# A two-layer MLP in Strassen form: one unit's split operands stay in SBUF, and the second product takes that unit first

## The chip, the cores and the metric

The kernel runs on one core of a Trainium2 chip. The time is the device time of one execution in microseconds (us), and less is better. The names of the engines in the profile are PE (TensorE's matmuls), PEld (its weight loads), DVE (VectorE), ACT (ScalarE), POOL (GpSimd) and SP (SyncE, which here only issues transfers).

## What is computed

One layer of a transformer trunk over 1024 tokens of width 1024, in float32. The part that this document is about is its last line but one, the MLP:

```python
mix = hybrid_mixer(x, w_in, b_f, pool_w, pool_scale, w_out)   # pooling heads and gated attention
x = layer_norm(ALPHA * x + mix, ln1_g, ln1_b)
hid = jnp.square(jax.nn.relu(x @ w_mlp1))                     # 1024 x 1024 by 1024 x 4096
x = layer_norm(ALPHA * x + hid @ w_mlp2, ln2_g, ln2_b)        # 1024 x 4096 by 4096 x 1024
```

## The kernel before

**Splits.** A float32 matrix is split into a high part in fp32r (a cast on ScalarE) and a low part (the rest, by a subtraction on VectorE); `split` at L70 does both, and a product is then three matmuls, high by high, high by low and low by high. In the profile L71 is the cast and L72 the subtraction.

**Seven products.** Both MLP products are done in two-by-two blocks with seven block products in place of eight, named p1 to p7 throughout. Each adds into one PSUM bank (`bank`, L63; banks have the tags s, pt, pv and mm). p1, p6, p7 and p4 of one unit or step run one after the other into the same bank and p5 and p3 into another, and between them the bank is emptied into SBUF, so that each next product must wait for that.

**The first product.** `Unit` u, 0 to 15, makes two column blocks of the hidden layer for both halves of the tokens. Its seven products have 12 matmuls each (128 x 128 by 128 x 512). It leaves four results in tiles of the tag A: `ra` and `rb` (after relu and square), and `sa` and `sb`, sums of them. `out_r` (L682) and `out_s` (L688) split these and write high and low parts to `hid_dram` from POOL's queue, seven writes of 512 KB a unit: the pair A12/A11, the pair S1/S2, the pair S3/S4 (two writes each, L680), and A22 (one, L686).

**The second product.** `Step` s is one of four quarters q = s % 4 of the tokens (128 of the first and 128 of the second half), and takes the hidden units in `TAKES[s]` (L851); every unit is taken once in each quarter. For a unit taken a product is three matmuls, so that a step with four units has seven products of 12 matmuls. `load` (L864) reads the units' operands of that quarter from `hid_dram` into tiles of the tags Q or A: three reads of 256 KB and one of 128 KB for each unit. `Pair` u holds the weights of unit u: two loads of 512 KB into tiles of the tag S (`load_f`, `load_g`), four sums on VectorE and seven splits into tiles of the tag B. Each step adds its products into `y` (`into`, L900): on the first four steps p1, p6, p5 and p4 are copied there by ScalarE (L903), and the rest, and all later ones, are added by VectorE (L905); p2 stays in a bank of its own to the last four steps. Before, steps 0, 1, 2 and 3 take 1, 2, 3 and 4 units, steps 4 to 11 four, and the last seven 3, 3, 3, 4, 4, 3 and 2; there are 19.

**Order.** The program writes the order out by hand: `chain` (L962) is units 2 to 15 and then the steps, and the loop at L1006 puts the products of one member (p1, p2, p6, p5) between those of the one before it (p7, p3, p4), so that unit 15's last three products lie among step 0's first four. `at(i, place, ...)` (L965) hangs loads, splits and outputs at places 0 to 7 of that order. The framework then sorts each engine's instructions by this order, and puts one forward where the engine would stand idle; it also gives out the slots. Each tag has a fixed number of them (L48: S 3, U 2, B 14, Q 10, A 9), and a tile waits until a slot's last user is done, which for a tile written to DRAM is the landing of the write. While the first product runs its operands `A[...]` fill all 14 B slots.

The numbers of the lines that the prediction speaks of: L895 the second product's matmul, L573 the first one's, L641, L646, L629 its evacuations by ScalarE, L657 to L664 its relu and square, L667 to L672 its sums, L677 and L678 the split of a result to be written, L874 the reads of `hid_dram`, L804 and L808 the loads of a pair.

Of the kernel before, what the change touches and what calls it, by code (L numbers as in the profile page):

```python
# [14 lines left out]
P = 128  # L15
# [9 lines left out]
NF = FF // P  # L25
# [9 lines left out]

@with_exitstack
def trunk(ctx, tc, xT, xn, wuqk, wvf, bf, poolw, pscale, wout, g1, b1, w1, w2, g2, b2, out):


# [11 lines left out]
    def slot(tag, shape, dt=F32R):  # L51
        uid[0] += 1
        return sb.tile([P] + list(shape), dt, tag=tag, bufs=NBUF[tag], name=f"{tag}{uid[0]}")
# [9 lines left out]
    def bank(tag=None):  # L63
        uid[0] += 1
        if tag is None:
            tag = CYCLE[rr[0] % 8]
            rr[0] += 1
        return ps.tile([P, CH], F32, tag=tag, bufs=PBUF[tag], name=f"{tag}{uid[0]}")

    def split(hi, lo, src):  # L70
        nc.scalar.copy(hi, src)  # L71
        nc.vector.tensor_tensor(lo, src, hi.bitcast(F32), ALU.subtract)  # L72
# [39 lines left out]
    def load_x(c, kp):  # L112
        st = slot("Q" if c == 0 else "S", [2, CH], F32)
        for k in range(2):
            if c == 0 and kp == 0:
                nc.sync.dma_start(st[:, k], xT[c, kp, :, k])
            elif k == 0:
                nc.sync.dma_start(st, xT[c, kp])
            if k == 0:
                x = slot("B", [2, 2, CH])  # L120
            t = x[:, k]
            split(t[:, 0], t[:, 1], st[:, k])
            xs[c, 2 * kp + k] = t
# [3 lines left out]
    def load_wvf(kp):  # L127
        st = slot("S", [2, 2 * VW], F32)
        hi, lo = slot("A", [2, 2 * VW]), slot("A", [2, 2 * VW])
        wv.append((hi, lo))  # L130
        if kp:
            nc.sync.dma_start(st, wvf[kp])
        for k in range(2):
            pieces = [slice(0, VW), slice(VW, 2 * VW)] if kp == 0 and k == 0 else [slice(0, 2 * VW)]
            for c in pieces:
                if kp == 0:
                    nc.sync.dma_start(st[:, k, c], wvf[kp, :, k, c])
                split(hi[:, k, c], lo[:, k, c], st[:, k, c])
                yield
# [22 lines left out]
    for kp in range(4):  # L162
        g = load_wvf(kp)
        if kp == 0:
            next(g)
        load_x(0, kp)
        for _ in g:
            pass
# [14 lines left out]
    for t in range(4, NT):  # L183
        for half in range(2):
            b = bank()[:, 0:VW]
# [274 lines left out]
    GROUPS = (("A12", "A11"), ("S1", "S2"), ("S3", "S4"), ("A22",))  # L460
# [14 lines left out]
    def load_row(tag, src):  # L475
        t = slot(tag, [D], F32)
        nc.sync.dma_start(t, src.to_broadcast([P, D]))
        return t

    class Norm:  # L480


        def __init__(self, y, gam, bet, store):
            self.y, self.gam, self.bet, self.store = y, gam, bet, store
            self.cols = [slice(0, CH), slice(CH, D)]
            self.st = small([P, 2, 6], "bns", bufs=4)
            self.mv, self.rt = small([P, 2], "mv", bufs=4), small([P, 5], "rt", bufs=4)
# [47 lines left out]
    A = {b: (slot("B", [H, CH]), slot("B", [H, CH])) for b in ("A11", "A12")}  # L535
    R0, R1, A22, raw22 = {}, {}, {}, {}
# [33 lines left out]
    def product(dst, b, a, first):  # L570
        for k in range(H):
            for i, (x, y) in enumerate(((0, 0), (0, 1), (1, 0))):
# [2 lines left out]
                    stop=k == H - 1 and i == 2, skip_group_check=not first,  # L575
                )

    class Unit:


        def __init__(self, u):
            self.u, self.v = u, {}

        def load_f(self):
            self.f = slot("S", [2, H, P], F32)
            nc.sync.dma_start(self.f.rearrange("p b k f -> p (b k) f"), w1[2 * self.u])
# [28 lines left out]
        def split_t2(self):  # L615
            v = slot("Q", [2, 1, H, P])
            self.keep(("T2",), v[:, 0], v[:, 1], self.t2.rearrange("p (o k) f -> p o k f", o=1))
# [55 lines left out]

        def out(self, name, x):

            hi = slot("A", [4, 2, P])
            nc.scalar.copy(hi, x)  # L677
            nc.vector.tensor_tensor(x, x, hi.bitcast(F32), ALU.subtract)  # L678
            for i, part in enumerate((hi.bitcast(F32), x)):
                nc.gpsimd.dma_start(hid_dram[self.u, :, i, AT[name] : AT[name] + 2 * CH], part.rearrange("p q n t -> p (q n t)"))  # L680

        def out_r(self):  # L682
            self.out("A12", self.ra)
            w = slot("A", [2, 4, P])
            split(w[:, 0], w[:, 1], self.rb[:, :, 1])
            nc.gpsimd.dma_start(hid_dram[self.u, :, :, AT["A22"] :], w.bitcast(F32).rearrange("p h q t -> p h (q t)"))  # L686

        def out_s(self):  # L688
# [3 lines left out]
    NU = NF // 2  # L692
    units = [Unit(u) for u in range(NU)]
    last = None
    for m in range(4):
# [13 lines left out]
        for t in (2 * m, 2 * m + 1):  # L709
# [11 lines left out]
            for n, part in enumerate(yp):  # L721
                ns = slice(n * CH, (n + 1) * CH)
                for k in range(KT):
                    a = mh[k // 4]
# [71 lines left out]
    class Pair:  # L796
# [29 lines left out]
            tt(f[:, 1], g[:, 1], f[:, 1], ALU.add)  # L826

        def split_t2(self):
            i = self.u % 4
            if self.u in (0, 2):  # L830
                t2b[i // 2] = slot("B", [2, 2, CH])
            w = t2b[i // 2][:, i % 2]
            self.put("T2", w[:, 0], w[:, 1], self.t2)
# [11 lines left out]
            self.both(("T4", "B22"), self.g)  # L845

    pairs = [Pair(u) for u in range(NU)]
    nh = [0]


    TAKES = [range(max(0, s - 3), s + 1) for s in range(12)]  # L851
    TAKES += [range(9, 12), range(10, 13), range(11, 14), range(12, 16), range(12, 16), range(13, 16), range(14, 16)]
    NS = len(TAKES)
    FIRST = [min(s for s in range(NS) if u in TAKES[s]) for u in range(NU)]

    class Step:


        def __init__(self, s):
            self.s, self.q, self.us = s, s % 4, list(TAKES[s])  # L860
            self.first, self.final, self.end = s < 4, s >= NS - 4, s == NS - 1
            self.h = {}

        def load(self, names):  # L864

            n = len(names)
            o = AT[names[0]] + self.q * n * P
            per = 4 // n
            for a in range(0, len(self.us), per):
                us = self.us[a : a + per]  # L870
                h = slot("A" if nh[0] >= 15 and (nh[0] - 15) % 11 > 7 else "Q", [per, 2, n, P])
                nh[0] += 1
                for e, u in enumerate(us):
                    nc.sync.dma_start(h[:, e].bitcast(F32).rearrange("p h n t -> p h (n t)"), hid_dram[u, :, :, o : o + n * P])  # L874
                    for k, name in enumerate(names):
                        self.h[u, name] = h[:, e, :, k]
# [4 lines left out]

        def load_x(self):

            self.t = self.s - 4
            self.xr = slot("S", [D], F32)
            nc.sync.dma_start(self.xr, x1_dram[self.t])

# [2 lines left out]

        def prod(self, dst, a, b, first):
            for u in self.us:
                h, w = self.h[u, a], pairs[u].v[b]
                for j, (p_, q_) in enumerate(((0, 0), (0, 1), (1, 0))):
                    nc.tensor.matmul(  # L895
                        dst, h[:, p_], w[q_], start=first and u == self.us[0] and j == 0,
                        stop=u == self.us[-1] and j == 2, skip_group_check=not first,
                    )
# [66 lines left out]
    def at(i, place, *fns):  # L965
        after.setdefault((i, place), []).extend(fns)

    for i, x in enumerate(chain):
        if isinstance(x, Unit):
            if x.u >= 4:  # L970
                at(i - 1, 0, x.load_f)
                at(i - 1, 2, x.load_g)
                at(i - 1, 3, x.split_f)
                at(i - 1, 4, x.sums)
                at(i - 1, 6, x.split_t2)
            if x.u >= 3:
                at(i, 1, x.split_t14)
                at(i, 4, x.split_t3b)
            at(i + 1, 7, x.sums_s)
            at(i + 2, 1, x.out_r)  # L980
            at(i + 2, 2, x.out_s)
        else:
            for k, p in enumerate(p for p in pairs if FIRST[p.u] == x.s):
                at(i - 1, 4 * k, p.load_f)
                at(i - 1, 2 + 3 * k, p.load_g)
                at(i - 1, 3 + 3 * k, p.split_b)
                at(i - 1 + k, 4 - 3 * k, p.sums)
                at(i - 1 + k, 5 - 4 * k, p.split_t2)
                at(i, 2 + k, p.split_t13)
                at(i, 6, p.split_t4b)  # L990
            if x.first:
                at(i - 1, 4, x.room)
            if 4 <= x.s < 12:
                at(i - 1, 6, x.load_x)
                at(i, 4, x.add_x)
            for n, place in enumerate((-4, -1, 0, 2) if 1 <= x.s < 4 else (-2, 0, 2, 4)):
                at(i + (place < 0) * -1, place % 7, lambda x=x, n=n: x.load(GROUPS[n]))
            if x.s == NS - 5:
                at(i + 1, 0, lambda: rows.update(gb=(load_row("S", g2), load_row("S", b2))))
# [59 lines left out]
```

## Time and profile before

| | us |
|---|---|
| median of 3 runs | 1069.94 (1068.82 to 1071.36) |
| profiled execution | 1071.98 |
| its span, first to last instruction | 1070.2 |
| TensorE busy | 1025.5 (96%) |
| VectorE busy | 772.9 (72%) |
| ScalarE busy | 499.9 (47%) |
| GpSimd busy | 119.6 (11%) |
| moved by DMA | 202.62 MB, of it 58.73 MB by POOL's queue |

A profile is one execution with every instruction's start and length. A line of it names the source line, the engine, the operation, and the tiles without their numbers, so `s<-B,Q` is a matmul into a bank of the tag s from a B tile and a Q tile. What stands in brackets is how long the engine had been idle before, and what it was waiting for. Matmuls overlap, so a group of 12 that shows 2.88 us starts 2.72 us before the next. MLP work runs from 420 to 1055 us of the span; the second product begins at 726.

### The profile page before, as it was taken

The page shows a single profiled execution, that of the slowest core. Times are in us where ns is not written, and L with a number is a line of the kernel's source. Part 1 is how long each engine was busy: PE and PEld are TensorE (multiplying, and loading weights), DVE is VectorE, ACT ScalarE, POOL GpSimd, SP SyncE. Part 2 cuts the span into 40 slices and gives each one's busy share as a digit, 9 for nine tenths or more (in the row PEclk, how much of TensorE's full clock was granted, in tenths as well). Part 3 has the DMA queues.
Part 4 walks back from the last instruction along what each step waited for, and adds up shares of the span by engine and source line. Part 5 has one row for each costly group of instructions (what it writes and reads, how often), then busy time and mean ns, then how long its engine had stood idle before and what let it go on. Part 6 is the DMA issues. An engine that isn't in the chain of part 4 may idle for free.

```text
span 1070.2 us, 14071 instructions
## 1 busy us (share of the span) xinstructions
PE 1025.5 (96%) x5006; PEld 849.4 (79%) x5006; DVE 772.9 (72%) x1308; ACT 499.9 (47%) x799; POOL 119.6 (11%) x188
## 2 busy tenths in 40 slices
PE   7999999999989999899999999998799999999994
PEld 7988787888768788688888888886688888888883
DVE  3576677777896798779788787888555575566568
ACT  4423666566773323476766667666422221122021
POOL 0000000000000021112122121221100000000055
PEclk9999999999999999899999999999899999999997
DMA  6303311021456532248667576679989888868852
GB/s 218 102 27 106 97 50 51 19 65 43 135 149 170 168 138 79 79 153 321 233 248 267 219 279 226 255 264 320 379 287 314 275 272 276 285 214 267 256 161 106
DMA packets 116726, 202.62 MB, mean 189 GB/s; under 512 B 9576, under 2 KB 82088, under 8 KB 116656
## 3 DMA queue, kind: packets, MB, share of 16 engines
q1 hardware_dynamic: 100528, 143.00, 41.7%
q0 software_dynamic: 16128, 58.73, 14.2%
q8 instruction: 39, 0.64, 0.3%
q14 instruction: 31, 0.25, 0.1%
HBM read 130.32 MB, written 71.37 MB: 188 GB/s over the span
## 4 chain that ended last, share of the span: by engine, by line
PE 77%; DVE 9%; DMA 7%; ACT 3%; issue 2%; SPq 0%; DVEq 0%; ACTq 0%
PE s L895 15%; PE s L573 11%; PE pv L895 7%; PE mm L573 6%; PE pt L573 6%; PE pv L573 4%; PE pv L384 3%; DMA Q<-hid_dram 3%; DMA S<-rin_dram 2%; PE mm L85 2%; PE mm L83 2%; PE mm L84 2%; PE pt L895 2%; PE mm L895 2%; PE s L83 2%
## 5 line engine op out<-in xcount | busy, mean ns | idle before, releaser
L71 ACT CAST B<-S 128x1024 fp32r<-128x1024 f32 (+1 forms) x94 | 80.1, 868 | 186.1 <-DMA S<-in_w_dram 75.9
L895 PE MATMUL s<-B,Q 128*128 128x512 f32 x579 | 142.8, 398 | 9.4 <-DMA Q<-hid_dram 9.4
L895 PEld LDWEIGHTS s<-B,Q 128*128 128x128 f32 x579 | 111.5, 193 | 34.2 <-DMA Q<-hid_dram 10.7
L72 DVE TENSOR_TENSOR B<-S,B 128x1024 fp32r<-128x1024 f32 (+1 forms) x94 | 92.5, 994 | 49.1 <-ACT B L71 48.8
L573 PE MATMUL s<-B,Q 128*128 128x512 f32 x504 | 122.0, 396 | 0.6 <-ACT B L71 0.6
L573 PEld LDWEIGHTS s<-B,Q 128*128 128x128 f32 x504 | 96.4, 191 | 21.7 <-ACT B L71 1.0
L71 ACT CAST Q<-S 128x1024 fp32r<-128x1024 f32 x53 | 55.5, 1050 | 65.6 <-PE s L573 16.6
L72 DVE TENSOR_TENSOR Q<-S,Q 128x1024 fp32r<-128x1024 f32 x53 | 64.6, 1220 | 25.9 <-ACT Q L71 25.7
L573 PE MATMUL mm<-B,Q 128*128 128x512 f32 x324 | 77.7, 390 | 0.0
L680 POOL DMA_DIRECT2D hid_dram<-A x96 | 51.4, 542 | 233.4 <-ACT A L677 195.9
L895 PE MATMUL pv<-B,Q 128*128 128x512 f32 x291 | 71.5, 390 | 0.3 <-ACT Q L903 0.3
L573 PEld LDWEIGHTS mm<-B,Q 128*128 128x128 f32 x324 | 60.7, 188 | 13.2 <-DVE Q L72 0.4
L573 PE MATMUL pt<-B,Q 128*128 128x512 f32 x288 | 68.7, 389 | 0.0
L384 PE MATMUL pv<-A,B 128*128 128x256 f32 x320 | 61.5, 297 | 5.2 <-ACT A L369 3.4
L384 PEld LDWEIGHTS pv<-A,B 128*128 128x128 f32 x320 | 49.1, 188 | 21.5 <-ACT A L369 9.1
L895 PEld LDWEIGHTS pv<-B,Q 128*128 128x128 f32 x291 | 54.5, 188 | 12.1 <-ACT Q L903 0.7
L573 PEld LDWEIGHTS pt<-B,Q 128*128 128x128 f32 x288 | 54.1, 188 | 11.2
L370 DVE TENSOR_TENSOR A<-pt,A 128x512 fp32r<-128x512 f32 (+1 forms) x80 | 49.2, 634 | 16.4 <-ACT A L369 15.8
L678 DVE TENSOR_TENSOR A<-A,A 128x1024 f32<-128x1024 f32 x48 | 57.0, 1217 | 3.4 <-ACT A L677 3.4
L347 ACT ACTIVATE A<-A,nm 128x128 f32<-128x128 f32 (+3 forms) x64 | 49.7, 777 | 20.9 <-DVE nm L345 20.6
L83 PE MATMUL mm<-B,B 128*128 128x512 f32 x120 | 51.7, 431 | 0.0
L369 ACT CAST A<-pt 128x512 fp32r<-128x512 f32 (+1 forms) x80 | 41.7, 539 | 17.0 <-PE pt L368 16.2
(360 smaller groups left out, 2180.6 us busy)
## 6 DMA issues: line engine op xcount, KB each, us to landing
hid_dram<-A POOLq DMA_DIRECT2D x112, 512.0 KB, 4.2
Q<-hid_dram SPq DMA_DIRECT2D x146, 256.0 KB
S<-in_w_dram SPq DMA_DIRECT2D x63, 512.0 KB
A<-hid_dram SPq DMA_DIRECT2D x46, 256.0 KB
S<-in_wuqk_dram SPq DMA_DIRECT2D x12, 512.0 KB
Q<-hid_dram SPq DMA_DIRECT2D x47, 128.0 KB
A<-ncf_dram SPq DMA_DIRECT2D x8, 512.0 KB
S<-in_wout_dram SPq DMA_DIRECT2D x8, 512.0 KB
```

The source lines that it names most:

```text
L71: nc.scalar.copy(hi, src)
L72: nc.vector.tensor_tensor(lo, src, hi.bitcast(F32), ALU.subtract)
L83: nc.tensor.matmul(dst, a[0], b[0], start=first, stop=False)
L84: nc.tensor.matmul(dst, a[0], b[1], start=False, stop=False)
L347: nc.scalar.activation(pt[:, :nk], pt[:, :nk], AF.Exp, bias=nm, scale=-1.0, accum_out=rsum[h][:, i : i + 1])
L369: nc.scalar.copy(tt[:, 0, ev], tp[:, ev])
L370: nc.vector.tensor_tensor(tt[:, 1, ev], tp[:, ev], tt[:, 0, ev].bitcast(F32), ALU.subtract)
L384: nc.tensor.matmul(ov, V[j][:, h].rearrange("p s d -> p (s d)"), tt[:, s, a:b], start=(j == 0 and s == 0), stop=(j == 2 * m + 1 and s == 1),)
L573: nc.tensor.matmul(dst, b[x][:, k], A[a][y][:, k], start=first and k == 0 and i == 0, stop=k == H - 1 and i == 2, skip_group_check=not first,)
L678: nc.vector.tensor_tensor(x, x, hi.bitcast(F32), ALU.subtract)
L680: nc.gpsimd.dma_start(hid_dram[self.u, :, i, AT[name] : AT[name] + 2 * CH], part.rearrange("p q n t -> p (q n t)"))
L895: nc.tensor.matmul(dst, h[:, p_], w[q_], start=first and u == self.us[0] and j == 0, stop=u == self.us[-1] and j == 2, skip_group_check=no ...
```

## The change

Unit 14 (`KEPT`) no longer writes to `hid_dram`. Its results are split straight into three B tiles (A12/A11, S1/S2, S3/S4) and one A tile (A22), which stay until step 3 is done. Its outputs are hung at earlier places: the split of `ra` behind unit 15's p6, the sums and A22 behind its own p4, the rest behind unit 15's p5, where before all three stood one to two places of the chain later. The second product takes unit 14 first, alone in steps 0 and 1 and with unit 0 in step 2 and units 0 and 1 in step 3; the others follow in the order 0 to 13 and 15, two steps later than before, so there are 20 steps: 1, 1, 2, 3, 3 units, then eight of 4 and the same seven at the end. The places that go by the number of the step (loads of the residual `x`, the early places of the loads, which loads use A slots, and the two shared tiles of the T2 splits) are shifted to fit.

```diff
+    KEPT = NF // 2 - 2
     class Unit:
         def __init__(self, u):
             self.u, self.v = u, {}
+            self.kept = {} if u == KEPT else None
...
         def out(self, name, x):
+            if self.kept is not None:
+                w = slot("B", [2, 4, 2, P])
+                split(w[:, 0], w[:, 1], x)
+                for n, one in enumerate(next(g for g in GROUPS if name in g)):
+                    self.kept[one] = w[:, :, :, n]
+                return
             hi = slot("A", [4, 2, P])
...
+        def out_a(self):
+            self.out("A12", self.ra)
+
         def out_r(self):
-            self.out("A12", self.ra)
+            if self.kept is None:
+                self.out_a()
             w = slot("A", [2, 4, P])
             split(w[:, 0], w[:, 1], self.rb[:, :, 1])
+            if self.kept is not None:
+                self.kept["A22"] = w
+                return
             nc.gpsimd.dma_start(hid_dram[self.u, :, :, AT["A22"] :], w.bitcast(F32).rearrange("p h q t -> p h (q t)"))
...
         def split_t2(self):
-            i = self.u % 4
-            if self.u in (0, 2):
+            i = nt2[0] % 4
+            nt2[0] += 1
+            if nt2[0] in (1, 3):
                 t2b[i // 2] = slot("B", [2, 2, CH])
...
-    TAKES = [range(max(0, s - 3), s + 1) for s in range(12)]
-    TAKES += [range(9, 12), range(10, 13), range(11, 14), range(12, 16), range(12, 16), range(13, 16), range(14, 16)]
+    ORDER = [u for u in range(NU) if u != KEPT]
+    TAKES = [[KEPT] * (s < 4) + ORDER[max(0, s - 5) : max(0, s - 1)] for s in range(13)]
+    TAKES += [ORDER[a:b] for a, b in ((8, 11), (9, 12), (10, 13), (11, 15), (11, 15), (12, 15), (13, 15))]
...
-            for a in range(0, len(self.us), per):
-                us = self.us[a : a + per]
-                h = slot("A" if nh[0] >= 15 and (nh[0] - 15) % 11 > 7 else "Q", [per, 2, n, P])
+            loaded = [u for u in self.us if u != KEPT]
+            for a in range(0, len(loaded), per):
+                us = loaded[a : a + per]
+                h = slot("A" if nh[0] >= 11 and (nh[0] - 11) % 11 > 7 else "Q", [per, 2, n, P])
...
-            self.t = self.s - 4
+            self.t = self.q + 4 * (self.s >= 9)
...
-                h, w = self.h[u, a], pairs[u].v[b]
+                h, w = units[KEPT].kept[a][:, :, self.q] if u == KEPT else self.h[u, a], pairs[u].v[b]
...
-            at(i + 1, 7, x.sums_s)
-            at(i + 2, 1, x.out_r)
-            at(i + 2, 2, x.out_s)
+            if x.kept is None:
+                at(i + 1, 7, x.sums_s)
+                at(i + 2, 1, x.out_r)
+                at(i + 2, 2, x.out_s)
+            else:
+                at(i + 1, 5, x.out_a)
+                at(i + 1, 6, x.sums_s, x.out_r)
+                at(i + 1, 7, x.out_s)
...
-            if 4 <= x.s < 12:
+            if 5 <= x.s < 13:
...
-            for n, place in enumerate((-4, -1, 0, 2) if 1 <= x.s < 4 else (-2, 0, 2, 4)):
+            for n, place in enumerate((-4, -1, 0, 2) if 2 <= x.s < 5 else (-2, 0, 2, 4)):
```

## Rows read from the trace of the kernel before

**Rows 1.** The page, part 2: TensorE's busy tenths in 40 slices of 26.75 us.

```profile
PE   7999999999989999899999999998799999999994
```

**Rows 2.** Waits of TensorE over the whole run: total us, times, longest us.

```profile
PE s L895 <- DMA Q<-hid_dram: 9.4, 3, 6.8
```

**Rows 3.** TensorE's timeline: start, us, line, what; in brackets the idle time before.

```profile
723.41 2.88 PE L573 MATMUL pt<-B,Q 128*128 128x512 f32 x12
726.13 0.84 PE L895 MATMUL s<-B,Q 128*128 128x512 f32 x3
...
736.50 0.84 PE L895 MATMUL pv<-B,Q 128*128 128x512 f32 x3
...
741.07 0.96 PE L895 MATMUL pv<-B,Q 128*128 128x512 f32 x3 [0.33 <-ACT Q L903]
...
752.23 6.07 PE L895 MATMUL s<-B,Q 128*128 128x512 f32 x15 [6.76 <-DMA Q<-hid_dram]
758.14 2.20 PE L895 MATMUL mm<-B,Q 128*128 128x512 f32 x9
...
767.46 0.96 PE L895 MATMUL s<-B,Q 128*128 128x512 f32 x3 [0.31 <-DMA Q<-hid_dram]
770.79 6.00 PE L895 MATMUL s<-B,Q 128*128 128x512 f32 x18 [2.37 <-DMA Q<-hid_dram]
776.63 2.89 PE L895 MATMUL mm<-B,Q 128*128 128x512 f32 x12
...
799.78 2.90 PE L895 MATMUL s<-B,A 128*128 128x512 f32 x12
```

**Rows 4.** Stretches: length, each engine's busy us, granted clock, DMA share, GB/s.

```profile
705.00:726.00 21.00, 21.00 (x94) 17.38 (x94) 17.16 (x23) 15.06 (x21) 3.88 (x7) 1.00 0.74 263
726.00:737.20 11.20, 11.20 (x51) 9.04 (x50) 11.20 (x16) 9.28 (x15) 2.84 (x6) 1.00 0.87 289
737.20:745.30 8.10, 7.77 (x34) 5.88 (x32) 8.06 (x13) 5.76 (x8) 1.54 (x3) 1.00 1.02 363
745.30:752.30 7.00, 0.24 (x2) 0.07 (x1) 3.56 (x4) 3.98 (x6) 2.53 (x5) 0.88 1.04 344
752.30:758.20 5.90, 5.90 (x16) 4.73 (x17) 1.98 (x4) 0.87 (x2) 0.82 (x2) 0.57 1.06 392
758.20:771.00 12.80, 10.12 (x44) 7.78 (x43) 5.85 (x8) 5.62 (x9) 0.00 (x0) 1.00 1.06 386
...
800.00:941.00 141.00, 141.00 (x622) 116.63 (x621) 87.11 (x119) 30.23 (x39) 0.00 (x0) 1.00 0.88 282
```

**Rows 5.** Chain that ended last, 735 to 800: start, us, what.

```profile
742.68 8.38 DMA Q<-hid_dram
...
751.68 12.90 DMA Q<-hid_dram
```

**Rows 6.** VectorE's timeline, 705 to 800, same columns as rows 3.

```profile
722.75 1.23 DVE L72 TENSOR_TENSOR B<-S,B 128x1024 fp32r<-128x1024 f32 x1 [1.84 <-ACT B L71]
...
729.37 0.68 DVE L671 TENSOR_TENSOR A<-A,A 128x512 f32<-128x512 f32 x1
...
743.05 0.68 DVE L905 TENSOR_TENSOR Q<-Q,pv 128x512 f32<-128x512 f32 x1
...
744.85 1.22 DVE L678 TENSOR_TENSOR A<-A,A 128x1024 f32<-128x1024 f32 x1
```

**Rows 7.** ScalarE's timeline, 705 to 800, same columns.

```profile
729.69 0.63 ACT L71 CAST B<-S 128x512 fp32r<-128x512 f32 x1
...
740.43 0.58 ACT L903 ACTIVATE Q<-pv 128x512 f32<-128x512 f32 x1
...
747.92 0.62 ACT L71 CAST B<-S 128x512 fp32r<-128x512 f32 x1 [4.96 <-DMA S<-in_w_dram]
```

**Rows 8.** hid_dram's transfers from 700 to 800, and the page's part 6 on its writes.

```profile
DMA to landing us min/median/max: 2.9/5.6/12.1
...
hid_dram<-A POOLq DMA_DIRECT2D x112, 512.0 KB, 4.2
```

More of the change, by code (lines that the diff above doesn't have):

```diff
@@ L847, in trunk @@
     pairs = [Pair(u) for u in range(NU)]
-    nh = [0]
-    TAKES = [range(max(0, s - 3), s + 1) for s in range(12)]
-    TAKES += [range(9, 12), range(10, 13), range(11, 14), range(12, 16), range(12, 16), range(13, 16), range(14, 16)]
+    nh, nt2 = [0], [0]
+    ORDER = [u for u in range(NU) if u != KEPT]
+    TAKES = [[KEPT] * (s < 4) + ORDER[max(0, s - 5) : max(0, s - 1)] for s in range(13)]
+    TAKES += [ORDER[a:b] for a, b in ((8, 11), (9, 12), (10, 13), (11, 15), (11, 15), (12, 15), (13, 15))]
     NS = len(TAKES)
```

## The prediction

> **What bounds the kernel now.** Read the page's slices first: of the forty slices of TensorE's row, thirty-four stand at 9, and slices 28 and 29 (722 to 776 us) at 8 and 7 are the only two neighbours that fall below it [rows 1]. So the time moves where TensorE still has holes. The list of TensorE's waits shows the largest one: the first matmuls of a product of the second MLP layer waiting for a load from hid_dram, 9.4 us in 3 waits, the longest 6.8 [rows 2]. TensorE's timeline then places it. From 723.41 on, 12 matmuls take 2.72 us, and this is the full rate. Step 0 of the second product begins at 726.13; the waits stand before 741.07, 752.23, 767.46 and 770.79; from 776.63 on TensorE runs without a hole [rows 3]. The table of stretches tells why: the DMA share is 1.02 to 1.06 from 737.2 to 771 at 344 to 392 GB/s, while in the quiet stretch from 800 to 941 it is 0.88 at 282 GB/s [rows 4]. The chain that ended last has two loads there of 8.38 and 12.90 us [rows 5]. Steps 0 to 3 take 1, 2, 3 and 4 units, all of them loaded within 45 us, together with the last writes of units 14 and 15: this is a bubble between two products, and it is bound by transfers.
>
> **What the bubble is worth.** Between 726.13 and 799.78 TensorE does 258 matmuls (36 that are left of unit 15, 21, 42 and 63 of steps 0 to 2, 72 of step 3, 24 of step 4). At 12 in 2.72 us these are 58.5 us; they took 73.65. So 15.2 us is the most that the change can win there. The parts: 6.76 + 2.37 + 0.33 + 0.31 = 9.8 us idle; 15 matmuls from 752.23 to 758.14 in 5.91 us in place of 3.40, so 2.5 us; 18 from 770.79 to 776.63 in 5.84 in place of 4.08, so 1.8 us [rows 3]; and 1.1 us in the modelled ends. The two slow groups are the clock: granted 0.57 of full speed in the stretch after the long wait [rows 4], so mostly the lower level of 1.2 GHz, after an idle stretch; everywhere else the upper one of 2.4.
>
> **Part by part.** *Matmuls*: the same 64 takes of 21 matmuls, so nothing. *Transfers removed*: unit 14's 7 writes (6 of 512 KB and one of 512 KB of its A22, 3.67 MB) and its 16 reads (12 of 256 KB, 4 of 128 KB, 3.67 MB). Steps 0 and 1 then load nothing, step 2 one unit, step 3 two. At the 386 GB/s of 758.2 to 771 [rows 4], the reads alone are 9.5 us of transfer in the stretch that is saturated. Steps 2 to 5 get their operands well ahead, since the Q slots come free at the same moments and SP has nothing queued in front of them but the weights of pairs 14 and 0. From step 5 on (four units a step) the demand is that of before, which was met without a wait at a DMA share of 0.88. I take the whole DMA wait as gone: **-15.2 us**.
>
> *Splits moved forward.* out_a, out_r and out_s of unit 14 go from one place later into the end of unit 15. Each is one cast on ScalarE and one subtraction on VectorE as before, 1.22 against 1.23 us [rows 6], so the work is equal and only its place counts. VectorE was busy 17.16 of 21 us from 705 to 726, and all of 11.20 after it [rows 4]. The A12/A11 split (1.2 us) fits the free 3.8; the S1/S2 split must be there by step 0's p6, some 6.8 us after p1 at 726.13. The sum it needs ended at 730.05 before [rows 6]; two splits behind each other end near 732. Cost 0 taken; if it comes after unit 15's work in the queue, up to 2 us late. The extra step adds 6 evacuations of 0.69 us [rows 6] = 4.1 us, hidden under VectorE's idle share of the second product (87.11 of 141 us busy [rows 4]); uncovered, it would cost those 4.1 at most.
>
> *A wait added: short products.* In steps 0 and 1 each product is 3 matmuls, 0.68 us. Step 0's p5 began at 736.50 [rows 3]; p3 of step 0 adds into the same bank, and now comes only three short products after p5's end, at 737.18 + 3 x 0.68 = 739.2. But ScalarE, which works on unit 15's relu and squares first, emptied that bank at 740.43, and p3 began at 741.07 [rows 3, 7]. That is 1.9 us. p5 of step 1 then needs the one pv bank again, which VectorE emptied from 743.05 to 743.74 [rows 6]; it would be due at 741.07 + 3 x 0.68 = 743.1: 0.6 more. Taken: **+2.4**, bounds 0 (another order on ScalarE) and 5 (each of the 8 evacuations from step 0's p6 to step 1's p5 exposed for its 0.6 us [rows 7]). The Trainium skill (Perfetto Trace Analysis, Matmuls) says that independent groups should rotate through different PSUM banks so that the evacuation of one overlaps the next; here p1, p6, p7 and p4 share one bank. By the rule alone all eight would be exposed, and the sum would be 2.4 us higher; the trace shows a 0.33 us wait for it in the old step 1, so I keep 2.4.
>
> *A wait added: A slots.* There are 9 A slots. In step 1 the kept A22 holds one that was free before, y1 and y5 two, unit 15 its four results and its split parts up to eight in all; y2 and y6, into which step 2 is emptied, must wait for one that a write to hid_dram frees. Before, step 2 began at 752.23 and found them free; now its p6 is due near 743.74 + 7 x 0.68 = 748.5. The low part of unit 15's first result was ready at 744.85 + 1.22 = 746.1 [rows 6], its write lands a median of 4.2 us later [rows 8], so 750.3, and 0.6 for the evacuation: 750.9. Taken: **+2.4**, bounds 0 (the framework puts other matmuls ahead) and 10.3 (the longest landing in this stretch, 12.1 us [rows 8]). Behind that evacuation on ScalarE stand the casts of pair 0's T1/T3 and step 2's other evacuations; behind p6 all of TensorE. By the fit in the Trainium skill (DMA: Bandwidth & Descriptors, Anatomy of one DMA), 2.0 us and bytes over 436 GB/s, a 512 KB write takes an estimated 3.2 us, and the sum would be 1 us lower; the trace's 4.2 decides.
>
> *Clock*: a wait of 2.4 us is most like the 2.37 us one, after which 1.8 us were lost. Taken **+1.8**, bounds 0 and the 2.5 after the long one.
>
> *Pair weights*: pair 0 now takes the old place of pair 1 in the S slots, whose second half was being cast at 729.69 [rows 7], some fifteen us before step 2. No cost; its cover is that lead. The wait of ScalarE for the next weights (4.96 us before 747.92 [rows 7]) belongs to the crowded queue and should shrink with it. The last steps take 4, 4, 3, 2 units as before, and the last 15 us after TensorE's end are untouched.
>
> **Sum.** -15.2 + 2.4 + 2.4 + 1.8 = -8.6 us. The profiled execution took 1071.98 us (span 1070.2), 2.0 above the median of 1069.94; 1063.4 against the profiled one, **1061.3 us** as a median.
>
> **Rivals.** *(a) The bubble closes wholly*: neither added wait bites, because the framework orders TensorE's instructions so that other products stand in between, and at most 1 or 2 us remain. 1054.7 to 1058.5. For it: the old trace's wait on an evacuation is only 0.33 us. Against: ScalarE's queue between 737 and 741. *(b) The A slots bite harder*: landings of 7 to 9 us in place of 4.2, 3 to 5 us more, and the splits up to 2 us late; 1064 to 1068. For it: 5.6 us is the median landing of all transfers of that table [rows 8]. *(c) Nothing is won*: the kept unit only moves the crowd to step 4, where three and then four units must be loaded at once, the waits of 6.8 and 2.4 return there with their clock loss, 1068 to 1072. Against it: the bytes are 3.67 MB fewer and step 4 begins some 25 us after unit 15's last operands leave their Q slots. *(d) Slower*: the A slot again. y2 waits for the landing of one write, and TensorE stands behind step 2's p6. At a landing of 12.1 us the terms are 2.4 + 10.3 + 2.5 = 15.2, all of the gain; this is the point from which it decides, and at 15 to 16 us it is some 3 us slower, 1073. Landings of that length need the saturated queue of before, whose loads are mostly gone. That the change fails to do what it says would show as steps 0 and 1 waiting for the splits; with up to 2 us this lies within (b).
>
> **How the numbers follow.** About 0.2% (2.1 us) is what a measurement of this kernel can tell from no change. Forecast, 1058.5 to 1064: 0.42. (a) 0.26. (b) 0.16. (c) 0.07, of which I count 0.06 as no change and 0.01 as faster. (d) 0.09. Faster: 0.42 + 0.26 + 0.16 + 0.01 = 0.85; same 0.06; slower 0.09. The range takes in the forecast, (a) to its end at 1069.94 - 15.2 = 1054.7, and (b) to 1068.
>
> **What would show it.** Right: no wait on hid_dram by TensorE between 720 and 800; DMA share under 1 there; the clock at its upper level, or one short dip; waits of TensorE on ScalarE or VectorE of 1 to 3 us in steps 0 to 2; the 4.96 us wait of ScalarE gone. The A-slot term is right if step 2's first evacuation starts when a write of unit 15 lands. Wrong: a new wait on loads at steps 4 or 5, a wait on the kept splits at step 0, or more than 15.2 us won, which would mean that time came from another stretch.

## The result, and the profile after

The changed kernel takes 1062.24 us (median of 4 runs, 1060.74 to 1062.45) against 1070.41 for the kernel before in the same runs: a ratio of 0.9921, with a 95% interval of 0.9907 to 0.9935. The profiled execution took 1062.45 us, 9.53 less than the one of before. Of that, 1.5 us lie ahead of step 0, which began at 724.61 and not at 726.13, behind the same matmuls in the same order. In the thirteen traces of this document step 0 begins at 723.16 to 727.58, so I count this as scatter and not as the change. From step 0's first matmul to the end of the span it is 336.1 us in place of 344.1, 8.0 less.

In the page, TensorE's slice 28 stands at 9 and slice 29 (now 742 to 769 us) at 8, where they stood at 8 and 7 [rows 1]; the second line is the writes' landing (columns as in [rows 8]).

```profile
PE   8999999999989999899999999999899999999994
...
hid_dram<-A POOLq DMA_DIRECT2D x105, 512.0 KB, 4.1
```

TensorE's waits: the line of [rows 2], 9.4 us on loads of hid_dram, is gone altogether. In its place stand one wait on an evacuation by ScalarE and two on casts of weights (the lines of the new source are some 21 higher: L916 is the old L895, L924 the old L903, L926 the old L905):

```profile
PE pv L916 <- ACT A L924: 1.9, 1, 1.9
...
PE s L916 <- ACT B L71: 0.7, 1, 0.7
PE mm L916 <- ACT B L71: 0.5, 1, 0.5
```

TensorE's timeline of the same stretch as [rows 3]:

```profile
724.61 0.84 PE L916 MATMUL s<-B,B 128*128 128x512 f32 x3
...
734.81 0.84 PE L916 MATMUL pv<-B,B 128*128 128x512 f32 x3
...
737.53 0.84 PE L916 MATMUL pv<-B,B 128*128 128x512 f32 x3
...
747.61 1.45 PE L916 MATMUL pv<-B,B 128*128 128x512 f32 x3 [1.94 <-ACT A L924]
748.85 1.05 PE L916 MATMUL s<-B,Q 128*128 128x512 f32 x2
749.71 1.48 PE L916 MATMUL s<-B,B 128*128 128x512 f32 x3
...
757.35 0.50 PE L916 MATMUL mm<-B,Q 128*128 128x512 f32 x1 [0.55 <-ACT B L71]
...
767.40 0.50 PE L916 MATMUL s<-B,Q 128*128 128x512 f32 x1 [0.66 <-ACT B L71]
768.12 0.74 PE L916 MATMUL s<-B,Q 128*128 128x512 f32 x2 [0.22 <-DVE B L72]
...
797.99 2.20 PE L916 MATMUL s<-B,Q 128*128 128x512 f32 x9
```

The stretches of [rows 4]:

```profile
726.00:737.20 11.20, 11.20 (x51) 9.29 (x50) 9.49 (x13) 9.51 (x13) 0.00 (x0) 1.00 0.36 122
737.20:745.30 8.10, 8.10 (x37) 6.37 (x35) 8.10 (x11) 7.48 (x12) 1.21 (x2) 1.00 1.09 354
745.30:752.30 7.00, 5.06 (x16) 3.71 (x15) 4.95 (x8) 1.48 (x3) 2.64 (x5) 0.76 1.04 408
752.30:758.20 5.90, 5.35 (x24) 4.00 (x23) 1.45 (x3) 3.03 (x6) 0.00 (x0) 1.00 0.77 291
758.20:771.00 12.80, 11.91 (x50) 8.99 (x49) 8.71 (x12) 5.80 (x9) 0.00 (x0) 1.00 0.71 228
```

Counted as in the prediction, the 294 matmuls from 724.61 to 797.99 lie 6.7 us over the full rate, where before it was 15.2. The hole at 747.61 is 2.1 us with its modelled end. The eight matmuls after it (747.61 to 750.99) start 0.42 us apart in place of 0.23, with a granted clock of 0.76 in that stretch: 1.7 us lost with the three behind them. The two waits on casts, at 757.35 and 767.40, cost 2.5 us with the small gaps around them (one of them the wait at 768.12 on VectorE). Some 0.4 us is scattered. From 726 to 737 the DMA share fell from 0.87 to 0.36 and the moved bytes from 289 to 122 GB/s, because steps 0 and 1 load nothing and unit 14 writes nothing. Behind that it is as full as before to 752.3, with shares of 1.09 and 1.04, and emptier after it, 0.77 and 0.71 in place of 1.06.

What held the evacuation is to be read on ScalarE (start, us, line, what, idle time before):

```profile
735.83 0.59 ACT L924 ACTIVATE Q<-pv 128x512 f32<-128x512 f32 x1
...
746.95 0.60 ACT L924 ACTIVATE A<-pv 128x512 f32<-128x512 f32 x1 [2.28 <-DMA hid_dram<-A]
748.24 0.60 ACT L924 ACTIVATE A<-s 128x512 f32<-128x512 f32 x1 [0.69 <-DMA hid_dram<-A]
...
756.68 0.62 ACT L71 CAST B<-S 128x512 fp32r<-128x512 f32 x1 [0.60 <-DMA S<-in_w_dram]
```

The copy at 746.95 goes from a pv bank into a tile of the tag A. It is p5 of step 1, into y5. ScalarE stood idle for 2.28 us until a write from an A tile to hid_dram had landed. So it is the wait for an A slot. The next copy, at 748.24, waits 0.69 us more for the next landing: it is the first evacuation of step 2, into y2. The chain that ended last goes the same way and further:

```profile
741.07 5.79 DMA hid_dram<-A
...
746.95 0.61 ACT A L924
...
747.58 0.69 DVE A L926
748.27 1.15 DVE B L72
...
749.47 7.19 DMA S<-in_w_dram
```

The first write of unit 15's results, the high part of A12/A11, is issued at 741.07 and lands after 5.79 us. Then y5 is filled, then VectorE's next addition runs, then a weight split that had stood behind it in VectorE's queue (748.27, T1 and T3 of pair 0). Then the S slot of pair 0's first block is free, and pair 1's second weight block is asked for, at 749.47. It lands 7.19 us later, and TensorE waits for its cast at 757.35, as it does for that of pair 2's first block at 767.40. So in this trace the waits hang together, through one slot and one queue.

### The profile page after: what moved, and what is told of

The parts are those of the page before. It is cut to its first block, busy times and chain, and to the rows that moved or that the text cites. A ratio compares the mean times of both kernels' runs of the same rounds, so it can differ in the third digit from the quotient of the medians.

```text
span 1060.7 us, 14042 instructions
## 1 busy us (share of the span) xinstructions
PE 1023.1 (96%) x5006; PEld 846.6 (80%) x5006; DVE 777.2 (73%) x1314; ACT 500.6 (47%) x799; POOL 115.2 (11%) x181
## 3 DMA queue, kind: packets, MB, share of 16 engines
q0 software_dynamic: 15120, 55.06, 13.4%
## 4 chain that ended last, share of the span: by engine, by line
PE 54%; issue 22%; DVE 9%; DMA 5%; POOL 5%; ACT 3%; SPq 0%; POOLq 0%; DVEq 0%; ACTq 0%
PE s L916 14%; PE pv L916 7%; POOL hid_dram L691 4%; PE pv L384 3%; PE mm L85 2%; PE mm L83 2%; PE mm L84 2%; DMA S<-rin_dram 2%; PE pt L916 2%; PE pt L368 2%; PE s L85 2%; PE mm L916 2%; PE s L573 2%; PE s L83 2%; PE s L84 2%
## 5 line engine op out<-in xcount | busy, mean ns | idle before, releaser
L916 PE MATMUL s<-B,Q 128*128 128x512 f32 x549 | 134.2, 391 | 1.3 <-ACT B L71 0.7
L916 PEld LDWEIGHTS s<-B,Q 128*128 128x128 f32 x549 | 103.5, 189 | 24.2 <-ACT B L71 1.1
L573 PE MATMUL s<-B,Q 128*128 128x512 f32 x504 | 120.9, 393 | 0.7 <-ACT B L71 0.7
L573 PEld LDWEIGHTS s<-B,Q 128*128 128x128 f32 x504 | 95.5, 190 | 21.4 <-ACT B L71 1.0
L691 POOL DMA_DIRECT2D hid_dram<-A x90 | 48.1, 538 | 234.7 <-ACT A L688 197.2
L916 PE MATMUL pv<-B,Q 128*128 128x512 f32 x273 | 67.0, 389 | 0.0
L916 PEld LDWEIGHTS pv<-B,Q 128*128 128x128 f32 x273 | 51.2, 188 | 10.7
L689 DVE TENSOR_TENSOR A<-A,A 128x1024 f32<-128x1024 f32 x45 | 53.4, 1217 | 0.0
```

Source lines behind the costliest of these rows:

```text
L573: nc.tensor.matmul(dst, b[x][:, k], A[a][y][:, k], start=first and k == 0 and i == 0, stop=k == H - 1 and i == 2, skip_group_check=not first,)
L916: nc.tensor.matmul(dst, h[:, p_], w[q_], start=first and u == self.us[0] and j == 0, stop=u == self.us[-1] and j == 2, skip_group_check=no ...
```

## The experiments

Two theories were set against each other. The **slots** theory: the 6.7 us that are left come from a shortage of A slots (y5 waits for a write) and of S slots (weights of pair 1 wait for a split of pair 0's). The **transfers** theory: the queues are full there (DMA share 1.09 and 1.04), and whatever slot is freed, TensorE waits for the next transfer. The first four kernels ran on one chip, beside 11 runs of the kernel before with a median of 1070.16 us, the next four on another beside 28 (1070.0), the last three on a third beside 11 (1069.86). So kernels of different groups are compared by their ratios. Beside a time I give what its trace shows from step 0's first matmul to the end of the span; this leaves out the scatter ahead of step 0, but it is one execution. It was 344.1 us before, and 336.1, 335.8 and 335.6 in the three traces of the changed kernel.

**The changed kernel once more.** No edit.

> The changed kernel once more, beside the others on one chip: 8 to 9 us under the kernel before, so that the other three can be set against it.

1062.18 us, ratio 0.9927 (0.9911 to 0.9943); 335.8 us from step 0 on, and 6.5 us over the full rate in the same stretch.

**The kept A22 in a Q slot.**

```diff
-            w = slot("A", [2, 4, P])
+            w = slot("A" if self.kept is None else "Q", [2, 4, P])
```

> The kept A22 lies in a Q slot, so one A slot more is free in steps 0 to 3. Theory (a shortage of A slots holds y5 back until a write of unit 15 has landed): TensorE's wait of 1.94 us on ScalarE goes, the slower clock after it too (1.7 us), and about 1 us of the late weights that stood behind it on VectorE: 3 to 5 us less than the changed kernel, unless the Q slot taken makes a load of step 4 late. Rival (the transfers themselves are late, DMA share 1.09 and 1.04 there): the wait moves to the next tile or to a load, within 1 us of the changed kernel.

1064.39 us, ratio 0.9945 (0.993 to 0.9961): not faster, but 2 us over the changed kernel, with intervals that overlap; 337.3 us from step 0 on, 1.2 to 1.7 over it. The theory's gain is missed. The rival had it right that the wait moves, though not that the time stays within 1 us. ScalarE's line shows where:

```profile
747.01 0.62 ACT L924 ACTIVATE A<-pv 128x512 f32<-128x512 f32 x1
749.29 0.60 ACT L924 ACTIVATE A<-s 128x512 f32<-128x512 f32 x1 [1.66 <-DMA hid_dram<-A]
...
759.75 0.62 ACT L71 CAST B<-S 128x512 fp32r<-128x512 f32 x1 [2.99 <-DMA S<-in_w_dram]
```

y5 (747.01) is filled without a wait. The next tile, y2 at 749.29, waits 1.66 us for a landing, and the cast of pair 1's second weight block waits 2.99 us; TensorE waited 2.94 for it. So one slot is one wait, as the theory has it, but the next tile stands in the line, and the weights are a cause of their own. Their block was asked for at 751.40, when an S slot came free, and took 8.32 us. Counted from step 0's start it landed at 32.1 us, just as in the changed kernel (756.66 less 724.61), though y5 was on time here: TensorE only came to that wait sooner.

**The kept A22 in two A slots.**

```diff
+            if self.kept is not None:
+                hi, lo = slot("A", [4, P]), slot("A", [4, P])
+                split(hi, lo, self.rb[:, :, 1])
+                self.kept["A22"] = (hi, lo)
+                return
             w = slot("A", [2, 4, P])
...
```

> The opposite dose: the kept A22 takes two A slots, one for each half. Theory: y5 or y1 waits for one landing more; the writes of unit 15 are issued 1.2 to 3.4 us apart, so TensorE's wait grows from 1.9 to 3 to 5 us and the time by 1 to 4 us over the changed kernel. Rival: the same time within 1 us.

1063.73 us, ratio 0.9937 (0.9923 to 0.9952), 1.5 us over the changed kernel, though the intervals overlap; 337.5 us from step 0 on. The trace is plainer than the time (L927 here is L924 elsewhere). ScalarE waits three times for a landing, and now even the split of unit 15's own result does:

```profile
748.18 1.04 ACT L688 CAST A<-A 128x1024 fp32r<-128x1024 f32 x1 [3.61 <-DMA hid_dram<-A]
749.77 0.60 ACT L927 ACTIVATE A<-pv 128x512 f32<-128x512 f32 x1 [0.55 <-DMA hid_dram<-A]
...
752.24 1.09 ACT L927 ACTIVATE A<-s 128x512 f32<-128x512 f32 x2 [1.87 <-DMA hid_dram<-A]
```

TensorE waited 2.8 + 0.6 us on these evacuations, against 2.2 in the trace of the changed kernel beside it. More A slots taken, more waiting.

**Pair 1's second weight block in a Q slot.**

```diff
-            self.g = slot("S", [2, CH], F32)
+            self.g = slot("Q" if self.u == 1 else "S", [2, CH], F32)
```

> The second weight block of pair 1 is loaded into a Q slot and no longer waits for the S slot that pair 0's last split frees at 749.4. Theory (the three waits of 0.2 to 0.7 us of steps 3 and 4 on casts come from weights that wait for S slots): the waits near 757 go, 1 to 2 us less than the changed kernel, the A-slot wait at 747 stays. Rival (weights are late because the transfer queue is full): no change, or a load of step 3 comes late and it is 1 to 2 us slower.

1060.96 us, ratio 0.9913 (0.9899 to 0.9928): 1.2 us less, which these intervals don't tell from nothing; 335.5 us from step 0 on, the same. In the trace both waits on casts are gone, and the one for the A slot stays, longer (the second row is at 793, out of the ramp):

```profile
PE pv L916 <- ACT A L924: 2.7, 1, 2.7
...
PE pv L916 <- DVE Q L926: 0.5, 1, 0.5
```

**The order alone**, through DRAM: unit 0 is taken where unit 14 was, and nothing is kept.

```diff
-    KEPT = NF // 2 - 2
+    KEPT = 0
...
-            self.kept = {} if u == KEPT else None
+            self.kept = None
...
-            loaded = [u for u in self.us if u != KEPT]
+            loaded = list(self.us)
```

(`prod` reads every unit's loaded operands, and the numbers by which loads take A slots and early places were set to fit.)

> The order of the change alone: unit 0 is taken alone in steps 0 and 1 and with one and two others in steps 2 and 3, but through DRAM as before; nothing is kept. Theory (the gain comes from the bytes that are gone from the stretch, 3.67 MB read and as many written): waits on hid_dram come back, at least 4 us of idle and slow clock more than in the changed kernel, 1066 to 1070. Rival (the gentler ramp of 1, 1, 2, 3, 3 units is enough, since it halves the loads per time as well): within 1.5 us of the changed kernel.

1069.62 us in 12 runs, ratio 0.9995 (0.9985 to 1.0006): no gain; 343.1 us from step 0 on, and 13.4 us over the full rate in the stretch. The waits on loads are back (total, times, longest), and so is the crowd in the stretches. The second row is a wait of step 0's p3 for the pv bank, with a short product:

```profile
PE s L916 <- DMA Q<-hid_dram: 8.6, 5, 4.1
...
739.47 0.97 PE L916 MATMUL pv<-B,Q 128*128 128x512 f32 x3 [0.68 <-ACT Q L924]
```

```profile
737.20:745.30 8.10, 4.08 (x17) 2.51 (x15) 8.07 (x12) 7.14 (x10) 1.60 (x4) 1.00 1.00 331
745.30:752.30 7.00, 5.62 (x17) 4.00 (x18) 2.73 (x4) 1.70 (x3) 2.29 (x4) 0.76 1.06 406
752.30:758.20 5.90, 3.19 (x14) 2.01 (x13) 2.49 (x4) 0.05 (x1) 0.00 (x0) 1.00 1.03 406
```

So the gentler growth of the steps brings no time that can be measured without the missing bytes.

**The unit kept, with the old growth** of 1, 2, 3 and 4 units, in 19 steps.

```diff
-    TAKES = [[KEPT] * (s < 4) + ORDER[max(0, s - 5) : max(0, s - 1)] for s in range(13)]
+    TAKES = [[KEPT] * (s < 4) + ORDER[max(0, s - 4) : s] for s in range(12)]
```

(with the places that go by the number of the step shifted back by one.)

> Unit 14 kept, but the steps grow as before: 1, 2, 3, 4 units, 19 steps. Steps 0 to 3 load 0, 1, 2, 3 units. Theory: the loads from DRAM are then no problem either, but the three B slots of the kept unit are missing for the weights of the third pair (3 + 4 x 3 + 2 of 14), so TensorE waits on casts of weights in steps 2 and 3: 1064 to 1070. Rival (keeping the operands is all that counts): within 1.5 us of the changed kernel or better, since there is a step less.

1067.36 us in 11 runs, ratio 0.9977 (0.9962 to 0.9992): some 2.5 us under the kernel before. The time is in the theory's range, but the place is so only in part: the wait on a cast is there (first row, TensorE's), yet the larger one is on a load of hid_dram. The last row is a third wait, at 839, with a slower clock behind it.

```profile
747.85 0.50 PE L916 MATMUL mm<-B,Q 128*128 128x512 f32 x1 [1.98 <-ACT B L71]
...
757.36 2.93 PE L916 MATMUL s<-B,Q 128*128 128x512 f32 x6 [4.22 <-DMA Q<-hid_dram]
...
PE pv L916 <- DVE A L926: 2.1, 1, 2.1
```

The chain that ended last shows how the load came late:

```profile
740.20 1.15 DVE B L72
...
741.36 0.33 SPq L826
...
745.70 11.62 DMA Q<-hid_dram
```

A weight load (L826) waits at the head of SP's queue for the S slot that a split frees at 741.35; the reads of hid_dram follow it one by one; and the one that TensorE needs, issued at 745.70, takes 11.62 us to land, at a DMA share of 1.04 to 1.05. So the bytes alone aren't enough either: with every loaded unit one step earlier, the loads queue up again. What the slot, SP's queue and the full transfers each had in it wasn't tried. That B slots ran out isn't seen. The profiled execution was one of the slowest of the 11 (1070.06 us, 344.1 from step 0 on); whether the others have the wait at 839 too isn't known.

**Unit 15's high parts in B slots**: three A slots fewer are taken while its results wait to be written.

```diff
-            hi = slot("A", [4, 2, P])
+            hi = slot("B" if self.u == NU - 1 else "A", [4, 2, P])
```

> The high parts of unit 15's three split results, which wait for their write to DRAM, lie in B slots instead of A slots; all else is as changed. Theory (A slots): with three A slots more from 738 on no evacuation waits for a landing; TensorE's wait of 1.9 to 2.2 us and the slow clock after it (1.7 us) go, the waits for weights (2.5 us with their clock) stay or grow by up to 1 us, as when A22 lay in a Q slot: 1059 to 1061. Rival (the waits only move from slots to transfers): within 1 us of the changed kernel.

1067.17 us in 12 runs, ratio 0.997 (0.9957 to 0.9982): a clear miss, some 5 us slower than the changed kernel; 339.8 us from step 0 on. No evacuation waits for a landing any more. Instead TensorE stands 5.6 us before 756.14 for a load of hid_dram, and 1.3 us at 773 for a cast of weights; the chain that ended last:

```profile
747.77 0.48 PE mm L916 x2
...
748.27 7.74 DMA Q<-hid_dram
...
756.14 2.47 PE s L916 x5
```

That load was issued only when a product in an mm bank let go of its slot at 748.25, and took 7.74 us. By this run alone the transfers theory would hold.

**Both: unit 15's high parts in B slots and pair 1's weights in a Q slot.** The two edits above together.

> Both: unit 15's high parts in B slots, and pair 1's second weight block in a Q slot. Theory: both terms are separate causes and both go; at most 2 us of the 6.7 between 724 and 800 are left, 4 to 5 us under the changed kernel: 1057 to 1059. Rival: with one wait gone another load or cast is late at once, and it stays within 2 us of the changed kernel.

1057.12 us, ratio 0.9884 (0.9866 to 0.9901); 331.6 us from step 0 on. It was run again beside the changed kernel:

> Unit 15's high parts in B slots and pair 1's second weight block in a Q slot, once more beside the changed kernel: 1056 to 1060, and its interval under that of the changed kernel.

> The changed kernel beside it, so that the two are compared on one chip: 1061 to 1063, with the wait of some 2 us on ScalarE in step 1 and the two late casts of weights as before.

1056.49 us, ratio 0.9878 (0.986 to 0.9896), and 1061.91 us, ratio 0.9929 (0.991 to 0.9947), for the changed kernel. The two intervals don't touch: 5.4 us less than the changed kernel, some 13 less than the one before. From step 0 on it is 331.6 us again, against 335.6. Only 1.8 us over the full rate are left of the 15.2. The stretches of this kernel, from the second of its traces:

```profile
737.20:745.30 8.10, 8.10 (x35) 6.25 (x35) 7.73 (x11) 7.03 (x11) 2.13 (x4) 1.00 1.01 336
745.30:752.30 7.00, 6.54 (x27) 4.23 (x25) 7.00 (x12) 4.30 (x7) 1.74 (x4) 1.00 1.05 412
752.30:758.20 5.90, 5.90 (x26) 4.90 (x27) 5.87 (x10) 4.36 (x7) 0.00 (x0) 1.00 1.05 395
758.20:771.00 12.80, 12.80 (x59) 10.58 (x58) 11.38 (x16) 6.30 (x9) 0.00 (x0) 1.00 0.93 306
```

From 745.3 to 758.2 the DMA share is 1.05 at 395 to 412 GB/s, as full as before the change (1.04 to 1.06), and the granted clock is 1.00 throughout, the upper level of 2.4 GHz. TensorE's one wait there, between 715 and 800:

```profile
PE s L916 <- DVE B L72: 0.5, 1, 0.5
```

This speaks for the slots, and against the transfers theory as it was stated: with the transfers as full as ever, TensorE waits for none of them once the slots are given out otherwise. It doesn't tell the slot itself from the order of SP's queue, which comes out otherwise with it.

**Kept A22 and pair 1's weights both in Q slots**: one A slot more in place of three.

> Kept A22 in a Q slot and pair 1's second weight block in another: one A slot more in place of three. Theory (both waits are about slots): no late weights; y5 is free at once, y2 still waits for a landing, 1 to 2 us with a clock dip of 0 to 1.7: 1059 to 1062. If the Q slots are what counts (two fewer for the loads of steps 3 and 4), waits on hid_dram of 2 us and more and 1063 to 1066.

1058.54 us, ratio 0.9895 (0.9878 to 0.9913), half a microsecond under the forecast; 332.7 us from step 0 on. TensorE's wait is the one foreseen, on y2's evacuation; it waits for no weights and, with two Q slots fewer, for no load either:

```profile
746.05 0.96 PE L916 MATMUL s<-B,B 128*128 128x512 f32 x3 [1.57 <-ACT A L924]
```

With the weights out of the way, the A22 slot is worth some 2 to 3 us: 1060.96 to 1058.54 on two chips, with intervals that overlap, and 335.5 to 332.7 from step 0 on. With them in the way it brought nothing.

What stays open: why high parts in B slots alone bring that late load, and the same with a Q slot fewer doesn't. SP's queue comes out in another order with an edit. In the kernel with B slots alone 14 reads of hid_dram stand ahead of pair 1's second weight block, in the other 4 stand before and 8 after. This order can't be the whole reason: the changed kernel has the same 14 ahead, and none of its loads was late. There the last of the 14 was issued 20.3 us after step 0's start, with B slots 24.2 us after. Outputs of the kept unit at their old places weren't tried either, since step 0 reads the splits before these places.

## Why the prediction was right, point by point

The time came out 0.9 us from the forecast of 1061.3. These were the terms of its sum, and the two that it took as nothing.

*Removed, 15.2 us.* Right: no wait of TensorE on hid_dram is left. The order alone (1069.62 us) and the kept unit with the old growth (1067.36 us) show that it needed both the order and the missing bytes, which the prediction didn't say; it spoke of the bytes and took the order as part of them.

*Splits moved forward, 0.* Right: step 0's matmuls on B tiles start without a wait from 724.61 on, one behind the other.

*Short products, +2.4.* Wrong: nothing. p5 of step 0 was emptied at 735.83, and p3 started at 737.53, exactly when its turn came (734.81 + 4 x 0.68). The step that failed is taking ScalarE's queue of before as that of after. There the pv bank was emptied at 740.43, behind unit 15's relu; now that relu starts at 733.29 in place of 737.10. Step 0's earlier start is 1.5 us of this. For the rest, the trace has no second pair's sums ahead of it on VectorE any more (before, pair 1's ran from 726.96 on; now pair 0's start at 733.89, behind it), which fits but wasn't tried alone. The mechanism itself is real: with the order alone, p3 of step 0 waited 0.68 us for this bank. The Trainium skill's rule on banks (Perfetto Trace Analysis, Matmuls) would have put even more here; the changed kernel shows no cost in these two steps.

*A slots, +2.4.* Right in mechanism; the size, 2.1 us, came out close partly by luck, and the tile that held TensorE was y5 of step 1, not y2 of step 2. The prediction counted y5 among the holders of slots, and its count (1, 2 and up to 8, for 9 slots) was over 9 already without y2. It let the low part's write free the slot, at 746.1, but the high part's goes first, at 741.07; the landing was longer, and TensorE needed the slot some 3 us sooner; these shifts nearly cancel. The landing took 5.79 us, not the median of 4.2. The estimate of 3.2 us from the Trainium skill (DMA: Bandwidth & Descriptors, Anatomy of one DMA) is further off in this crowd. The sign named beforehand came: step 2's first evacuation, into y2, starts at 748.24 when a write lands. With A22 in a Q slot y2 holds TensorE too, its own wait 1.66 us.

*Clock, +1.8.* Right: 1.7 us after the 1.94 us wait, by the same reading as [rows 3].

*Pair weights, 0.* Wrong: 2.5 us. Pair 0's weights did come early, as forecast. The step that failed is stopping there. The next block, pair 1's second, waits for the S slot that pair 0's split frees, and takes 7.19 us to land. That the wait for an S slot makes it late is borne out: with the block in a Q slot both waits on casts are gone. In the trace the split stood on VectorE behind an addition that waited for y5; the prediction named what was queued on ScalarE behind y2's evacuation, but not on VectorE. How much this queue adds isn't shown, since with A22 in a Q slot y5 is on time and the block lands no sooner.

So the sum held (6.7 us left against 6.6) by luck in part: two errors of 2.4 and 2.5 us cancelled. Of the signs named beforehand, the DMA share was one too many: it didn't stay under 1 (1.09, 1.04), where the reads for steps 2 and 3 now stand together with unit 15's writes. Rival (a), the bubble closing wholly, is what the kernel with both edits does, 1057. Rival (d) was near in kind: the kernel with two slots taken waited longer for landings, though its 1.5 us over the changed kernel lie within the intervals.

## What to carry to other kernels

When operands stay in SBUF to spare a crowded stretch, count the slots that they take away, tag by tag, and name the next two tiles of each tag, not one. Of slots that bind together, freeing one kind may bring nothing or cost time, while freeing both pays: here A slots alone cost 2 us (not clear of the noise) and 5 us, the weights' slot alone brought at most 1.2, and both brought 5.4. Try pairs before dropping either. A DMA share of 1.0 says that a stretch is full, not that it is what TensorE waits for; see which slot or queue issued the late transfer. Once late, a transfer in such a stretch lands late too: 7.2 to 11.6 us after its issue in the chains above.

## What was not expected of the hardware

TensorE ran without a clock dip through 13 us at a DMA share of 1.05 and up to 412 GB/s, well over the 282 GB/s of the long quiet stretch [rows 4]. A write of 512 KB to DRAM took 5.79 us to land in that crowd, though 105 of them had a median of 4.1.
